# A hybrid decoder layer on one core: VectorE's order fixed by hand between the output projection and the FFN's block sums

## Chip, cores, metric

The kernel runs on one core of one Trainium2 chip. The metric is the device time of one execution in microseconds (us). Engines are named as in the profile: PE is TensorE (matmuls), PEld its weight loads, DVE is VectorE, ACT is ScalarE, POOL is GpSimd, SP is SyncE, whose only work here is to start DMAs. ACTq and SPq are the DMAs that those engines start.

## The reference

One layer of a decoder over 1024 prompt tokens and 8 x 4 sample tokens. Cut to what matters here:

```python
h = rmsnorm(x, g_pre); p = h @ w_in              # all mixers' columns in one projection
# ya: gated short conv, yb: windowed attention, yc: chunked spatial gate
merged = g[:, :, 0] * (ya @ w_ba) + g[:, :, 1] * (yb @ w_bb) + g[:, :, 2] * (yc @ w_bc)
x = x + rmsnorm(merged @ w_o, g_post)            # output projection, second norm, residual
up = rmsnorm(x, g_pre_f) @ w_up                  # FFN
upc, ffn_new = causal_dwconv(up, ffn_prev, conv_f_w, conv_f_b)
fa, fb = jnp.split(upc, 2, axis=-1)
x = x + rmsnorm((jax.nn.silu(fa) * fb) @ w_down, g_post_f)
```

`rmsnorm(x, g)` is `x * rsqrt(mean(x*x) + 1e-6) * g`. The model width is 1024, the FFN's inner width 2816, all in float32.

## The kernel before

Features lie on the 128 partitions, tokens along the free dimension: 1056 tokens (1024 + 32), cut into three chunks `c` of 352. `M8` holds eight feature tiles of 1056 tokens in float32. Every product is made of three matmuls of rounded values: each operand is split into a high part (a rounded copy, made by ACT) and a low part (the rest, a subtraction on DVE); `H` holds the 8 high and 8 low tiles of the activations. Weights come in blocks of 4 tiles (128 x 512): SP loads a block into a `raw` buffer (three of these), ACT copies it, DVE subtracts. Up-projection weights of the first FFN columns go into slots of `Y`, which hold output-projection weights until PE is through with these.

The place in question is the passage from the output projection to the FFN:

- For each chunk, the output projection makes eight tiles `n`, 24 matmuls each. `evac_o` lets ACT move a tile out of PSUM (scaled by `g_post`) and square it; DVE adds up the squares.
- `chain(c, ...)` is then the whole norm, residual and second norm of chunk `c`. It is a generator that is advanced by one step after every 12 matmuls of the following work. Its parts: `rstd_of` adds squares over partitions with small matmuls against `ones` (tile `aux`); `factor_of` scales the sums on DVE and raises them to -1/2 on POOL (tile `rs`, 88x4); `spread` sends these back over the partitions by four transposes on PE, and ACT copies the result (`rs`, later `R`). Then, for pairs of tiles n = 0, 2, 4, 6: DVE multiplies `M` by `rs`, DVE adds the residual `xr` (loaded from `in_x`), ACT squares, DVE adds the squares to `acc2`, and the sum goes to DRAM (`x2d`). A second `rstd_of` reads `acc2`; after its `spread` DVE scales by `g_pre_f` and `R`, ACT copies to `H`, DVE subtracts.
- Chunk 0's chain runs beside chunk 1's output projection, chunk 1's beside chunk 2's. Chunk 2's runs beside the first FFN products (`up_unit` for j = 0 and 1), with tiles cut out of the `cz` buffers in place of its own, and with two residual buffers. Chunk 1 of the FFN products follows chunk 0, then chunk 2.
- `combos(X, p)` makes the block sums for the Strassen products of the later FFN columns (sums of quarters of `M`, four high and four low parts in `Y`), for two halves p of the tokens. `act_pair(j)` is the convolution, the SiLU and the product of FFN column pair j. Weights of the Strassen columns are loaded into `M` when the block sums are through with it.

PE's order is the order in which the program is written. The order of the other engines, and of the DMAs on each queue, is chosen by a scheduler from its own estimate of the times; each engine then runs its row strictly in that order, and a row's wait holds everything behind it.

## Time and profile before

| | us |
|---|---|
| runs (three) | 1490.8, 1488.62, 1488.98 |
| median | 1488.98 |
| profiled execution | 1487.42 |
| its span in the profile | 1485.6 |

The span runs from the first to the last instruction; 1.8 us of the profiled execution lie around it. "PE aux L100" is the group of small matmuls of `rstd_of`, "PE aux L306" the transposes of `spread`. A timeline row reads: start, duration of the group, engine, line, operation, out<-in, shape, count, and in brackets the idle time of the engine before it and what ended it. A row of the view by stretches gives the stretch, its length, busy time and instruction count of PE, PEld, DVE, ACT and POOL, then the granted clock of PE (1.00 is full speed), the busy share of the DMA engines and GB/s.

### The profile page before, as it was taken

The numbers are of one execution on the slowest core, as the hardware profiler recorded it, in microseconds if no ns is written. First come the engines' busy times: TensorE is split into PE (matmuls) and PEld (weight loads), VectorE is DVE, ScalarE is ACT, GpSimd is POOL, SyncE is SP. The second block draws the span as 40 slices with busy tenths as digits, with TensorE's granted clock in tenths as the row PEclk, the third lists the DMA queues.
The fourth block names the chain that finished last, engine by engine and source line by source line (L and its number), as shares of the span: only waits on it lengthen the run. The fifth ranks groups of instructions, "written<-read, shape, count | busy, mean of one in ns | idle before, by whom it ended". The sixth has DMA issues, their size and how long they took to land.

```text
span 1485.6 us, 25718 instructions
## 1 busy us (share of the span) xinstructions
PE 1434.6 (97%) x10163; PEld 1424.2 (96%) x10163; DVE 900.3 (61%) x1603; ACT 658.0 (44%) x1338; POOL 251.2 (17%) x319
## 2 busy tenths in 40 slices
PE   4899999999999999999889999999999999999997
PEld 3899999999999999999889999999999999999997
DVE  6844445325777546755678677777777783453546
ACT  5444444445766322243436454555454574121333
POOL 2100000012455215410013022122122210000000
PEclk9999999999999999999999999999999999999998
DMA  6222333211001236642340122221222174231215
GB/s 231 77 91 96 102 108 109 91 55 36 30 30 36 59 119 181 188 141 79 122 138 38 57 81 80 87 80 66 79 80 80 54 261 148 73 109 43 86 39 151
DMA packets 77833, 141.40 MB, mean 95 GB/s; under 512 B 8256, under 2 KB 34816, under 8 KB 77696
## 3 DMA queue, kind: packets, MB, share of 16 engines
q1 hardware_dynamic: 66192, 112.94, 24.0%
q10 hardware_dynamic: 11520, 26.82, 4.7%
q8 instruction: 80, 1.31, 0.4%
q14 instruction: 41, 0.34, 0.1%
HBM read 105.58 MB, written 35.16 MB: 95 GB/s over the span
## 4 chain that ended last, share of the span: by engine, by line
PE 90%; DVE 3%; ACT 2%; issue 2%; POOL 1%; DMA 1%; SPq 0%; POOLq 0%; DVEq 0%; ACTq 0%
PE mm L100 54%; PE wb L100 20%; PE aux L100 13%; POOL rs L301 1%; DVE M L94 1%; PE sp L100 1%; ACT M L686 1%; DMA M<-in_x 1%; PE aux L699 1%; DVE M L680 0%; DMA raw<-in_wu 0%; DVE Y L97 0%; PE aux L306 0%; DVE H L97 0%; DVE acc L94 0%
## 5 line engine op out<-in xcount | busy, mean ns | idle before, releaser
L100 PE MATMUL mm<-Y,wh 128*128 128x264 f32 (+1 forms) x1824 | 364.2, 295 | 0.0
L100 PE MATMUL mm<-H,wh 128*128 128x352 f32 (+1 forms) x1568 | 354.5, 313 | 1.5 <-DVE Y L97 0.9
L100 PEld LDWEIGHTS mm<-Y,wh 128*128 128x128 f32 x1824 | 292.3, 189 | 0.0
L100 PE MATMUL mm<-Y,wl 128*128 128x264 f32 (+1 forms) x912 | 268.7, 295 | 0.0
L100 PEld LDWEIGHTS mm<-H,wh 128*128 128x128 f32 x1568 | 261.6, 188 | 2.5 <-PE aux L100 1.1
L100 PE MATMUL mm<-H,wl 128*128 128x352 f32 (+1 forms) x784 | 243.5, 311 | 0.0
L100 PEld LDWEIGHTS mm<-Y,wl 128*128 128x128 f32 x912 | 171.2, 188 | 0.0
L91 ACT ACTIVATE wh<-M 128x512 fp32r<-128x512 f32 x126 | 79.6, 632 | 155.0 <-PE aux L100 67.4
L100 PE MATMUL wb<-H,wh 128*128 128x264 f32 (+1 forms) x720 | 147.6, 298 | 0.0
L100 PEld LDWEIGHTS mm<-H,wl 128*128 128x128 f32 x784 | 147.2, 188 | 0.0
L91 ACT ACTIVATE wh<-raw 128x512 fp32r<-128x512 f32 (+1 forms) x98 | 58.2, 594 | 169.3 <-PE mm L100 109.6
L1035 DVE SCALAR_TENSOR_TENSOR cz<-U,cst,cz 128x1072 f32<-128x1072 f32 x88 | 113.9, 1329 | 13.4 <-ACT cz L1033 13.3
L100 PEld LDWEIGHTS wb<-H,wh 128*128 128x128 f32 x720 | 116.3, 188 | 0.0
L100 PE MATMUL mm<-H,Y 128*128 128x352 f32 x624 | 109.4, 335 | 2.6 <-DVE H L97 2.6
L97 DVE TENSOR_TENSOR wl<-M,wh 128x512 fp32r<-128x512 f32 x126 | 86.4, 686 | 39.0 <-ACT wh L91 39.0
L100 PEld LDWEIGHTS mm<-H,Y 128*128 128x128 f32 x624 | 105.4, 196 | 3.0 <-DVE H L97 3.0
L100 PE MATMUL wb<-H,wl 128*128 128x264 f32 (+1 forms) x360 | 107.2, 298 | 0.0
L97 DVE TENSOR_TENSOR wl<-xraw,wh 128x512 fp32r<-128x512 f32 x70 | 48.5, 692 | 90.0 <-ACT wh L91 89.5
L301 POOL TENSOR_TENSOR rs<-rs,nhalf 88x4 f32<-88x4 f32 (+2 forms) x12 | 24.7, 2055 | 395.7 <-DVE rs L300 395.7
L94 DVE TENSOR_TENSOR M<-M 128x512 f32<-128x512 f32 (+1 forms) x88 | 69.5, 790 | 26.7 <-DMA M<-in_wu 25.9
L94 DVE TENSOR_TENSOR M<-mm,M 128x352 f32<-128x352 f32 (+3 forms) x79 | 39.5, 505 | 76.0 <-PE mm L100 76.0
L97 DVE TENSOR_TENSOR wl<-raw,wh 128x512 fp32r<-128x512 f32 (+1 forms) x72 | 52.7, 733 | 52.3 <-ACT wh L91 52.3
(219 smaller groups left out, 2636.2 us busy)
## 6 DMA issues: line engine op xcount, KB each, us to landing
M<-in_wu SPq DMA_DIRECT2D x72, 256.0 KB, 2.6
sig<-sigd SPq DMA_DIRECT2D x72, 176.0 KB, 2.9
y2d<-cz ACTq DMA_DIRECT2D x22, 528.0 KB, 2.8
sigd<-M ACTq DMA_DIRECT2D x40, 264.0 KB, 3.3
xraw<-in_win SPq DMA_DIRECT2D x40, 256.0 KB, 2.7
raw<-in_wd SPq DMA_DIRECT2D x40, 256.0 KB, 2.7
raw<-in_win SPq DMA_DIRECT2D x39, 256.0 KB, 2.6
Y<-y2d SPq DMA_DIRECT2D x14, 528.0 KB, 6.6
```

Source lines behind the costliest of these rows:

```text
L91: act.activation(out, in_, AF.Copy)
L94: return eng.tensor_tensor(out, a, b, op=op)
L97: eng.tensor_tensor(out, a, b, op=ALU.subtract)
L100: pe.matmul(out, lhsT, rhs, start=start, stop=stop, skip_group_check=more)
L301: pool.tensor_tensor(v, v, nhalf[:bs, :nb], op=ALU.pow)
L686: act.activation(s[:, h, :], s[:, h, :], AF.Exp, bias=ng[:, h : h + 1], scale=SCALE, accum_out=l[:, h : h + 1])
L699: pe.transpose(pt[:, h * P : (h + 1) * P], s[:, h, kb * P : (kb + 1) * P], ident)
L1035: dve.scalar_tensor_tensor(z, u[:, s : s + CONV], cwf[:, f, s : s + 1], z, ALU.mult, ALU.add)
```

## The change

From the output projection until the second half of the block sums, DVE's instructions stand in the order in which the program is written, as PE's do already. With that, the written order is altered in a few places: `combos` becomes a generator in four pieces, of which the first half's two pieces fill the places behind the two `rstd_of` of chunk 2, and the rest comes after that chain; `act_pair(1)` comes after the second half. Behind each power on POOL a DVE copy (`ru`) is made, and the transposes read the copy. The residual of chunks 0 and 1 is loaded into four buffers ahead of the chunk's products; in chunk 2 the later two residual loads, and all the stores to `x2d`, go out on ACT's queue. Squares are made per tile (352) and not per pair (704), and the buffers `sq` and `sq2` go from two to one.

```diff
@@ combos
             tt(b11, b12, b11, ALU.subtract)
             tt(b12, b22, b12, ALU.subtract)
+            yield
             tt(b22, b22, b11, ALU.subtract)
             part(1, b22)
+            yield
             part(0, b11)
             part(2, b12)
+            yield
             tt(b21, b21, b22, ALU.subtract)
             part(3, b21)
@@ factor_of
             pool.tensor_tensor(v, v, nhalf[:bs, :nb], op=ALU.pow)
+            if hold[0]:
+                u = fixed.tile([P, 4], F32, name="ru", bufs=2)[:bs, :nb]
+                dve.tensor_copy(u, v)
+                v = u
@@ evac_o
-                    sq = pc.tile([P, CW], F32, name="sq", bufs=2)
+                    sq = pc.tile([P, CW], F32, name="sq", bufs=1)
...
-                        sums[c] = pc.tile([P, 2, CW], F32, name="sq2", bufs=2)
+                        sums[c] = pc.tile([P, 2, CW], F32, name="sq2", bufs=1)
@@ chain
-            load_xr(0)
-            load_xr(2)
+            queue = nc.sync if c < 2 else nc.scalar
             yield
             spread = rstd_of(acc, rs)
+            next(fill, None)
...
-                tt(m, m, xr[n // 2 % 2], ALU.add)
-                load_xr(n + 4)
-                if n == 0:
-                    act.activation(acc2, m, AF.Square)
-                elif type(sq) is list:
+                tt(m, m, xr[n // 2], ALU.add)
+                queue.dma_start(x2d[:, n : n + 2, cc(c)], m)
+                if c == 2 and n < 4:
+                    load_xr(c, n + 4, xr[n // 2], queue)
+                for q in range(2):
+                    if n == 0:
+                        act.activation(acc2[:, q, :], m[:, q, :], AF.Square)
+                    else:
+                        act.activation(sq[q], m[:, q, :], AF.Square)
+                if n:
                     for q in range(2):
-                        act.activation(sq[q], m[:, q, :], AF.Square)
                         tt(acc2[:, q, :], acc2[:, q, :], sq[q], ALU.add)
-                else:
-                    act.activation(sq, m, AF.Square)
-                    tt(acc2, acc2, sq, ALU.add)
-                nc.sync.dma_start(x2d[:, n : n + 2, cc(c)], m)
...
             spread = rstd_of([acc2[:, 0, :], acc2[:, 1, :]], R[:, cc(c)])
+            next(fill, None)
...
         steps = []
+        order = ExitStack()
+        order.enter_context(tc.manual_schedule(engines={mybir.EngineType.DVE}))
+        hold[0] = True
         for c in CHUNKS:
+            if c < 2:
+                xr = [pc.tile([P, 2, CW], F32, name="xr", bufs=4) for _ in range(4)]
+                for n in range(0, 8, 2):
+                    load_xr(c, n, xr[n // 2])
...
-                    if c == 2:
+                    if c == 2 and j == 0:
                         act_pair(j)
-            combos(M8, 1)
+            drain(combos(M8, 1))
+            act_pair(1)
+            order.close()
+            hold[0] = False
```

Scaling and splitting for `H` is also written one pair ahead (`scale(n + 2)` before the subtraction of pair n).

What the engines' rows become is shown at three places. First, DVE in chunk 1's chain. Before (`Y<-raw,Y` is the subtraction of a weight block, `R<-R,sq` a sum of chunk 2's squares, `acc` here the second sum of squares):

```order
L94 TENSOR_TENSOR M<-M,rs 128x2x352 x4
L97 TENSOR_TENSOR Y<-raw,Y 128x512
L94 TENSOR_TENSOR M<-M,xr 128x2x352 x2
L97 TENSOR_TENSOR Y<-raw,Y 128x512
L94 TENSOR_TENSOR R<-R,sq 128x352
L97 TENSOR_TENSOR Y<-raw,Y 128x512
L94 TENSOR_TENSOR acc_7577<-acc_7577,sq_7578 128x704
L94 TENSOR_TENSOR M<-M,xr 128x2x352
```

The same place after the change:

```order
L94 TENSOR_TENSOR M<-M,rs 128x2x352
L94 TENSOR_TENSOR M<-M,xr 128x2x352
L97 TENSOR_TENSOR Y<-raw,Y 128x512 x2
L94 TENSOR_TENSOR M<-M,rs 128x2x352
L94 TENSOR_TENSOR M<-M,xr 128x2x352
L94 TENSOR_TENSOR acc_7599<-acc_7599,sq_7597 128x352 x2
L94 TENSOR_TENSOR R<-R,sq 128x352
L94 TENSOR_TENSOR M<-M,rs 128x2x352
L94 TENSOR_TENSOR M<-M,xr 128x2x352
L94 TENSOR_TENSOR acc_7599<-acc_7599,sq_7597 128x352 x2
L97 TENSOR_TENSOR Y<-raw,Y 128x512 x2
```

Each pair is finished before the next begins, and the first two weight subtractions, which stood ahead of the chain, stand behind its first pair.

Second, ACT at the end of that chain, after the change (`sq_7597<-M` are the squares of pairs n = 4 and n = 6, `M<-mm` and `sq<-mm` chunk 2's tiles):

```order
L941 ACTIVATE sq_7597<-M 128x352 x2
L898 ACTIVATE M<-mm,cst 128x352
L91 ACTIVATE Y<-raw 128x512
L941 ACTIVATE sq_7597<-M 128x352 x2
L91 ACTIVATE wh<-raw 128x512
```

A weight block's copy stands ahead of the last pair's squares. Third, DVE in chunk 2's chain; before (`M<-M 128x4x264` and `Y<-M,Y` belong to the block sums, `M<-M 128x512` to later weights):

```order
L97 TENSOR_TENSOR Y<-M,Y 128x1056
L94 TENSOR_TENSOR M<-M 128x4x264
L97 TENSOR_TENSOR Y<-M,Y 128x1056
L94 TENSOR_TENSOR M<-M,cz 128x2x352 x4
L97 TENSOR_TENSOR Y<-M,Y 128x1056
L94 TENSOR_TENSOR M<-M,cz 128x2x352 x2
L94 TENSOR_TENSOR M<-M 128x512
L94 TENSOR_TENSOR cz<-cz 128x352
```

and after:

```order
L310 TENSOR_SCALAR rs<-aux 88x4
L314 COPY ru<-rs 88x4
L94 TENSOR_TENSOR M<-M 128x4x264 x2
L94 TENSOR_TENSOR M<-M,cz 128x2x352 x4
L94 TENSOR_TENSOR cz<-cz 128x352 x2
L94 TENSOR_TENSOR M<-M,cz 128x2x352 x2
L94 TENSOR_TENSOR cz<-cz 128x352 x2
L97 TENSOR_TENSOR wl<-raw,wh 128x512
L94 TENSOR_TENSOR M<-M,cz 128x2x352 x2
L94 TENSOR_TENSOR cz<-cz 128x352 x2
```

Only two block sums stand ahead of the chain, and its four rows `M<-M,cz ... x4` are now multiply, add, multiply, add, where they were four multiplications.

## The prediction

> **What bounds the kernel now.** I read the page first, then who waited for whom on PE between 690 and 800 us, then PE's timeline there with the granted clock, and last the rows of DVE, ACT and the DMAs ahead of each wait.

> ```profile
> PE 1434.6 (97%) x10163; PEld 1424.2 (96%) x10163; DVE 900.3 (61%) x1603; ACT 658.0 (44%) x1338; POOL 251.2 (17%) x319
> ```

> PE is the bound. The change gives PE the same row of instructions as before, so it can only move PE's waits, and the clock behind them. In the stretch it touches these are:

> ```profile
> PE aux L100 <- DVE acc L94: 4.6, 2, 3.9
> PE aux L100 <- issue: 3.8, 1, 3.8
> PE aux L100 <- DVE R L94: 0.2, 1, 0.2
> ```

> That is 8.55 us, all in front of the matmuls against `ones`. In PE's timeline:

> ```profile
> 693.45 1.41 PE L100 MATMUL aux<-ones,acc 128*88 128x1 f32 x16 [0.66 <-DVE acc L94]
> ...
> 709.25 4.12 PE L100 MATMUL wb<-H,Y 128*128 128x352 f32 x24
> ...
> 725.22 2.10 PE L100 MATMUL wb<-H,Y 128*128 128x352 f32 x12
> 731.22 2.48 PE L100 MATMUL aux<-ones,acc 128*88 128x1 f32 x16 [3.90 <-DVE acc L94]
> 733.56 6.13 PE L100 MATMUL wb<-H,Y 128*128 128x352 f32 x24
> ...
> 762.67 5.99 PE L100 MATMUL mm<-H,Y 128*128 128x352 f32 x36
> 772.41 2.60 PE L100 MATMUL aux<-ones,cz 128*88 128x1 f32 x16 [3.75 <-issue]
> 774.88 5.97 PE L100 MATMUL mm<-H,Y 128*128 128x352 f32 x24
> ```

> The waits of 0.66, 3.90 and 3.75 us belong to the second sums of chunks 0, 1 and 2. The reader is to see also what follows the long ones: the 16 small matmuls take 2.48 and 2.60 us where 1.41 do behind the short wait, the 24 matmuls behind them 6.13 and 5.97 us where 4.12 do. The clock says why:

> ```profile
> 734.00:736.00 2.00, 2.00 (x8) 2.00 (x8) 0.00 (x0) 0.00 (x0) 0.97 (x1) 0.50 0.07 25
> ...
> 776.00:778.00 2.00, 2.00 (x9) 2.00 (x8) 0.00 (x0) 0.00 (x0) 0.37 (x1) 0.50 0.00 0
> ```

> In these stretches, behind both long waits, PE ran at 0.50 (the third last column); behind the wait of 0.66 us the 16 small matmuls took 1.41. So each long wait cost its length and a slow stretch: 1.07 + 2.01 = 3.08 us for chunk 1, 1.19 + 1.85 = 3.04 for chunk 2. All that can be won here is 8.55 + 6.12 = 14.7 us; PE has no other wait in this passage.

> **Chunk 0's chain.** Its last sum was 0.66 us late. With the pairs finished one by one and all residuals loaded ahead, the last pair's sum follows the last square with nothing queued between; I count the wait as gone: 0.66 us won (between 0 and 0.66).

> **Chunk 1's chain.** The rows that set its pace:

> ```profile
> 715.15 3.29 DVE L94 TENSOR_TENSOR M<-M,rs 128x704 f32<-128x704 f32 x4
> 718.36 0.69 DVE L97 TENSOR_TENSOR Y<-raw,Y 128x512 fp32r<-128x512 f32 x1
> 718.96 1.69 DVE L94 TENSOR_TENSOR M<-M,xr 128x704 f32<-128x704 f32 x2
> ...
> 724.87 0.89 DVE L94 TENSOR_TENSOR M<-M,xr 128x704 f32<-128x704 f32 x1 [1.77 <-DMA xr<-in_x]
> 763.91 0.87 ACT L926 ACTIVATE cz<-M 128x352 f32<-128x352 f32 x2
> 768.95 0.96 DVE L94 TENSOR_TENSOR cz<-cz 128x352 f32<-128x352 f32 x2 [0.62 <-ACT cz L926]
> 722.32 0.63 ACT L91 ACTIVATE Y<-raw 128x512 fp32r<-128x512 f32 x1
> raw<-in_wu SPq DMA_DIRECT2D x9, 256.0 KB, 3.6
> DMA to landing us min/median/max: 2.4/3.6/6.4
> ```

> Before, the chain lost 1.77 us to a residual that landed late; the four buffers take that away. But the new order puts waits in its place. A multiplication or addition of a pair takes 0.82 us (3.29 / 4), so 1.64 a pair; a weight subtraction 0.60 (718.36 to 718.96); a residual sum of chunk 2 0.44; and from a finished addition to finished squares and their sums it is half of the 0.87, the 0.96 and the hand-overs, 1.5 us. In the row before, DVE filled these 1.5 us with the next pair. Now it stands still in them, three times. And two more things queue up. The first weight subtractions stood ahead of the chain, in DVE's idle time, and now stand behind the first pair; the buffer that they free is the one into which SP loads weight block 5, whose copy ACT makes ahead of the squares of pair 2. In the same way the copy of block 7 stands ahead of the squares of pair 6, and its load waits for a subtraction that follows the sums of pair 4.

> With loads of 2.4 us (the shortest) the times are: start 715.2, as before; pair 0 ends 716.8; two weight subtractions, 718.0, the first of them at 717.5 frees the buffer; block 5 lands 719.9, is copied by 720.5; squares and sums of pair 2 by 722.0; sum of chunk 2, 722.4; pair 4, 724.0; its sums 725.5; weight subtraction 726.1, block 7 lands 728.5, copied 729.1; pair 6 was added by 728.4, so its squares start at 729.1 and the sums end at 730.6. With the median of 3.6 us for both loads it is 1.2 us more at each, 733.1. PE is free at 727.3 (725.22 + 2.10), so it waits 3.3 to 5.8 us; I take the middle, 4.6, against 3.90 before: 0.7 lost. That is long enough for the clock to fall as it did before, so nothing is won behind it.

> **The first sum of chunk 2** (0.24 us, the row of 0.2 above) waited for DVE's last sum of squares, behind block sums. These are now behind it: 0.2 won.

> **Chunk 2's chain.**

> ```profile
> 754.56 0.47 PE L306 MATMUL aux<-ident,rs 88*128 88x88 f32 x4
> 755.11 0.46 ACT L91 ACTIVATE cz<-aux 128x352 f32<-128x352 f32 x1
> 756.89 3.29 DVE L94 TENSOR_TENSOR M<-M,cz 128x704 f32<-128x704 f32 x4
> 760.10 1.24 DVE L97 TENSOR_TENSOR Y<-M,Y 128x1056 fp32r<-128x1056 f32 x1
> 761.27 1.68 DVE L94 TENSOR_TENSOR M<-M,cz 128x704 f32<-128x704 f32 x2
> 749.86 0.36 ACTq L973 DMA_DIRECT2D sff<-in_sff  x1
> cz<-in_x SPq DMA_DIRECT2D x4, 352.0 KB, 5.0
> ```

> Before, `rs` was there at 755.57, the first multiplication began at 756.89, and the first additions, which free the residual buffers, at 761.27, behind four multiplications and a block sum; the loads behind them then took 5.0 us, in the company of the weight loads. Now pair 0 is multiplied and added by 755.6 + 1.64 = 757.2. Stores and residual loads cost ACT an issue each, 0.36 us by the one ACT issue shown: load 4 leaves by 758.0 and, even at 5.0 us, is there at 763.0. Pair 2 is added by 758.9, but ACT has two issues and pair 0's squares (0.72 + 0.87) first, to 758.8, then its own two issues: squares start at 759.7, sums end at 761.2. Pair 4: added by 763.8 (load 763.0, addition 0.82); one store, squares, sums: 0.36 + 1.5, 765.7. A weight subtraction, pair 6, a store, squares and sums: 0.6 + 1.64 + 0.36 + 1.5, so 769.8. PE is free at 768.7 (762.67 + 5.99): a wait of about 1.2 us where 3.75 stood, between 0 (the load in less than 5.0 us, which the weight loads no longer crowd since the block sums that free their room come later) and 2.9 (ACT's copies of block sums and evacuations each in front). That is 2.55 won, and at 1.2 us the clock stays up, as it did after 0.66: 3.04 more.

> **The rest**, at nothing, with its cover. The copies behind the powers: 24 matmuls lie between the small matmuls and the transposes, 4.12 us by the row of 709.25, and

> ```profile
> 775.37 1.00 POOL L301 TENSOR_TENSOR rs<-rs,nhalf 88x4 f32<-88x4 f32 x1 [17.54 <-DVE rs L300]
> ```

> the power takes 1.00 of them, so a copy of some tenths is in time; DVE, which stands for that 1.00 in front of the copy, has only what the sums above contain behind it. The block sums moved behind chunk 2's chain: four rows of 1.24 for the first half and eight for the second, 15 us, and two convolution pairs. behind the second transposes of chunk 2 PE still has 12 + 24 matmuls of chunk 1, 96 of chunk 2 and 144 of FFN column 2 before the first Strassen product needs them, 276 at 4.12 per 24, some 45 us, and DVE is busy 61% of its time; without that cover each us late would be one on PE.

> **The sum:** 0.66 - 0.7 + 0.2 + 2.55 + 3.04 = 5.75 us. Against the profiled execution, 1487.42, this is 1481.7. The median of the runs is 1.56 us above that execution, so against the median 1488.98 it is 1483.2. What a measurement can tell from no change here is 0.2%, 3.0 us.

> **Rivals.**

> The clock. Each of two waits above 3.7 us brought it down, none below 0.7 did; the rows show nothing between. If chunk 1's wait comes out near 3.3 us and the clock holds, 3.08 more is won: 1480.1. For it speaks the shortest load, against it that both waits near that length did fall. [...]

> The wait moves, and nothing is won. Chunk 1 at its far end, 5.8 us, chunk 2 at 2.9 with the 16 small matmuls behind it slow enough that the clock falls again: 5.8 + 3.08 + 2.9 + 3.04 = 14.8, just what is lost now, 1489.0; with only the clock of chunk 2 falling, 1486.2. For it speaks that ACT now has evacuations, copies, issues and squares of chunk 2 in one row.

> Slower: the weights of chunk 0's output projection.

> ```profile
> 641.96 0.80 SPq L906 DMA_DIRECT2D xr<-in_x  x2
> 650.82 11.84 PE L100 MATMUL mm<-H,Y 128*128 128x352 f32 x72
> 652.68 0.63 ACT L91 ACTIVATE Y<-raw 128x512 fp32r<-128x512 f32 x1 [0.37 <-DMA raw<-in_wo]
> ```

> Tile 3's matmuls end at 654.75 (a third of 11.84 after 650.82) and tile 5's begin at 658.7. The sum of tiles 2 and 3 (an addition of 704, 0.89 as in the row of 724.87) now stands in front of the weight subtractions for tile 5, and needs tile 3's square, about 1.0 after its end (two ACT rows of about half a us, as 0.46 above): 655.8 + 0.9 + 0.69 = 657.4, a margin of 1.3 us; for tile 7 it is the same again. Ahead of all this SP starts four residual loads, not two, 704 KB more in front of the weights. The margin is gone once ACT's copies, which stand ahead of tile 3's evacuation and wait for loads, are 1.3 us late. Late by 5 us, it would be 3.7 us at tile 5, with a slow clock of 3.1 behind, and some 2 at tile 7: 8.8 lost, 1483.2 + 8.8 = 1492. It decides from 5.75 us on. Against it speaks that the copies wait 0.37 us only for a load at 652.68.

> **Chances.** The forecast, chunk 2's wait mostly gone and chunk 1's kept: 0.52, by its own bounds (3.3 to 5.8, 0 to 2.9) 1480.7 to 1486. The clock holds at chunk 1: 0.16, near 1480. The wait moves: 0.21, 1486 to 1489. Slower: 0.11. Left out on both sides is a fifth at most with 1478.5 to 1489.5. Faster by over 0.2% (below 1486.0) are the first two and a quarter of the third: 0.73. Within 0.2%: the rest of the third and a little of the last: 0.17. Slower: 0.10.

> **What would show it.** After the change the second sum of chunk 0 should have no wait; that of chunk 1 a wait of 3.3 to 5.8 us behind DVE's `acc`, a clock of 0.50 after it, and ACT's last squares there directly behind a `Y<-raw` copy that waits for `raw<-in_wu`; that of chunk 2 a wait under 3 us with the clock at 1.00 behind it. PE should have no wait for `H`, `Y` or `wl` from 640 to 830 us. The prediction is wrong if chunk 1's wait is under 2.5 us (the weight loads then don't hold the squares), if chunk 2's stays above 3, or if a new wait stands in the output projection of chunk 0 or at the first Strassen product.

## The result and the profile after

Beside the first runs of the changed kernel the kernel before took 1488.8 us (median of 4 runs) and the changed kernel 1479.8 (4 runs, 1479.45 to 1479.92), a ratio of 0.9942 with a 95% interval of 0.9927 to 0.9957. In a second lot, timed beside the experiments, it took 1482.09 us (6 runs, 1479.99 to 1484.15) against 1488.79: 0.9955, 0.9941 to 0.9969. So it is 6.7 to 9.0 us faster, where 5.75 were forecast. What was expected of the second lot, ahead of it: a median of 1480 to 1483 with a spread of several us if the 1479.8 us were in part luck of those four runs, all runs within 1 us of 1479.8 if not. The first came out. The profiled execution took 1479.45 us with a span of 1477.7; that of before had 1487.42.

TensorE's row on the page after, and who waited for whom on PE from 640 to 830 us (total, times, longest):

```profile
PE 1430.0 (97%) x10163; PEld 1419.4 (96%) x10163; DVE 903.0 (61%) x1615; ACT 659.0 (45%) x1347; POOL 248.4 (17%) x319
```

```profile
PE aux L100 <- DVE acc L94: 4.9, 2, 4.7
PE aux L100 <- issue: 0.6, 1, 0.6
```

PE's timeline, at the places that the prediction showed of before:

```profile
673.27 0.71 PE L100 MATMUL aux<-ones,acc 128*88 128x1 f32 x8
...
691.72 1.51 PE L100 MATMUL aux<-ones,acc 128*88 128x1 f32 x16
...
707.41 0.76 PE L100 MATMUL aux<-ones,acc 128*88 128x1 f32 x8 [0.24 <-DVE acc L94]
...
730.75 2.56 PE L100 MATMUL aux<-ones,acc 128*88 128x1 f32 x16 [4.68 <-DVE acc L94]
733.17 5.93 PE L100 MATMUL wb<-H,Y 128*128 128x352 f32 x24
...
748.94 0.71 PE L100 MATMUL aux<-ones,R 128*88 128x1 f32 x8
...
761.55 5.98 PE L100 MATMUL mm<-H,Y 128*128 128x352 f32 x36
768.18 1.64 PE L100 MATMUL aux<-ones,cz 128*88 128x1 f32 x16 [0.64 <-issue]
769.68 4.13 PE L100 MATMUL mm<-H,Y 128*128 128x352 f32 x24
```

The second sum of chunk 0 has lost its wait of 0.66 us. Chunk 1's wait has grown from 3.90 to 4.68, with slow matmuls behind it as before (2.56 and 5.93 us). Chunk 2's has shrunk from 3.75 to 0.64, and the 24 matmuls behind it take 4.13 us where they took 5.97: the clock stayed up. The wait of 0.24 us at the first sum of chunk 2 is gone, and one of the same length stands at the first sum of chunk 1. In the clock's view (PEclk is the third last column) the slow stretch behind chunk 1 is still there and the one behind chunk 2 is not:

```profile
734.00:736.00 2.00, 2.00 (x9) 0.50 0.49 164
...
776.00:778.00 2.00, 2.00 (x14) 1.00 0.00 0
```

Chunk 1's chain ahead of the long wait, first on ACT's timeline, then on DVE's:

```profile
729.03 0.63 ACT L91 ACTIVATE Y<-raw 128x512 fp32r<-128x512 f32 x1 [3.50 <-DMA raw<-in_wu]
729.57 0.87 ACT L941 ACTIVATE sq<-M 128x352 f32<-128x352 f32 x2
```

```profile
730.08 0.96 DVE L94 TENSOR_TENSOR acc<-acc,sq 128x352 f32<-128x352 f32 x2 [1.45 <-ACT sq L941]
```

The last squares stand directly behind a weight copy that waited 3.50 us for its load, the sums follow, and PE's small matmuls begin right behind these.

### The profile page after: what moved, and what is told of

Read it like the earlier page. It is cut to its first block, busy times and chain, and to the rows that moved or that the text cites. A ratio compares the mean times of both kernels' runs of the same rounds, so it can differ in the third digit from the quotient of the medians.

```text
span 1477.7 us, 25715 instructions
## 1 busy us (share of the span) xinstructions
PE 1430.0 (97%) x10163; PEld 1419.4 (96%) x10163; DVE 903.0 (61%) x1615; ACT 659.0 (45%) x1347; POOL 248.4 (17%) x319
## 4 chain that ended last, share of the span: by engine, by line
PE 90%; DVE 4%; ACT 2%; issue 2%; POOL 1%; DMA 1%; ACTq 0%; SPq 0%; POOLq 0%; DVEq 0%
PE mm L100 54%; PE wb L100 20%; PE aux L100 13%; DVE M L94 1%; POOL rs L311 1%; PE sp L100 1%; ACT M L700 1%; PE aux L713 1%; DMA M<-in_x 1%; DVE M L694 0%; DMA raw<-in_wu 0%; DVE acc L94 0%; DVE Y L97 0%; ACT Y L91 0%; PE aux L320 0%
## 5 line engine op out<-in xcount | busy, mean ns | idle before, releaser
L100 PE MATMUL mm<-Y,wh 128*128 128x264 f32 (+1 forms) x1824 | 363.8, 295 | 0.0
L100 PE MATMUL mm<-H,wh 128*128 128x352 f32 (+1 forms) x1568 | 354.3, 313 | 1.5 <-DVE Y L97 0.9
L100 PEld LDWEIGHTS mm<-Y,wh 128*128 128x128 f32 x1824 | 292.6, 188 | 0.0
L100 PE MATMUL mm<-Y,wl 128*128 128x264 f32 (+1 forms) x912 | 269.4, 295 | 0.0
L100 PEld LDWEIGHTS mm<-H,wh 128*128 128x128 f32 x1568 | 261.6, 188 | 2.5 <-PE aux L100 1.1
L100 PE MATMUL mm<-H,wl 128*128 128x352 f32 (+1 forms) x784 | 243.7, 311 | 0.0
L100 PEld LDWEIGHTS mm<-Y,wl 128*128 128x128 f32 x912 | 171.8, 188 | 0.0
L100 PE MATMUL wb<-H,wh 128*128 128x264 f32 (+1 forms) x720 | 147.7, 298 | 0.0
L91 ACT ACTIVATE wh<-M 128x512 fp32r<-128x512 f32 x126 | 79.5, 631 | 152.8 <-PE aux L100 65.9
L100 PEld LDWEIGHTS mm<-H,wl 128*128 128x128 f32 x784 | 147.3, 188 | 0.0
L91 ACT ACTIVATE wh<-raw 128x512 fp32r<-128x512 f32 (+1 forms) x98 | 58.3, 594 | 169.2 <-PE mm L100 110.6
L100 PEld LDWEIGHTS wb<-H,wh 128*128 128x128 f32 x720 | 116.4, 188 | 0.0
L100 PE MATMUL mm<-H,Y 128*128 128x352 f32 x624 | 107.2, 331 | 2.6 <-DVE H L97 2.6
L100 PE MATMUL wb<-H,wl 128*128 128x264 f32 (+1 forms) x360 | 107.3, 298 | 0.0
L97 DVE TENSOR_TENSOR wl<-M,wh 128x512 fp32r<-128x512 f32 x126 | 86.5, 686 | 32.8 <-ACT wh L91 32.8
L100 PEld LDWEIGHTS mm<-H,Y 128*128 128x128 f32 x624 | 103.1, 192 | 3.0 <-DVE H L97 3.0
L97 DVE TENSOR_TENSOR wl<-xraw,wh 128x512 fp32r<-128x512 f32 x70 | 48.5, 693 | 90.3 <-ACT wh L91 89.8
L94 DVE TENSOR_TENSOR M<-mm,M 128x352 f32<-128x352 f32 (+3 forms) x79 | 39.5, 506 | 76.2 <-PE mm L100 76.2
L94 DVE TENSOR_TENSOR M<-M 128x512 f32<-128x512 f32 (+1 forms) x88 | 69.5, 790 | 27.1 <-DMA M<-in_wu 26.3
L97 DVE TENSOR_TENSOR wl<-raw,wh 128x512 fp32r<-128x512 f32 (+1 forms) x72 | 53.0, 737 | 51.7 <-ACT wh L91 51.7
## 6 DMA issues: line engine op xcount, KB each, us to landing
M<-in_wu SPq DMA_DIRECT2D x72, 256.0 KB, 2.6
xraw<-in_win SPq DMA_DIRECT2D x40, 256.0 KB, 2.7
raw<-in_wd SPq DMA_DIRECT2D x40, 256.0 KB, 2.6
raw<-in_win SPq DMA_DIRECT2D x39, 256.0 KB, 2.6
```

What stands on the lines that cost most here:

```text
L91: act.activation(out, in_, AF.Copy)
L94: return eng.tensor_tensor(out, a, b, op=op)
L97: eng.tensor_tensor(out, a, b, op=ALU.subtract)
L100: pe.matmul(out, lhsT, rhs, start=start, stop=stop, skip_group_check=more)
```

## The experiments

The runs share one table. "Stretch" is the time from the start of chunk 0's first sum to that of the kernel's last sum of squares on PE: 674.12 to 1474.32 before, 673.27 to 1466.74 after. It leaves out what happens ahead of it, and with that the output projection of chunk 0, where weights can come late (see the rivals below). A lot is one chip: versions 1 to 4 ran on one, the second lot with 5, 6 and 8 on another, 4 again with 7 and 9 on a third, 10 on a fourth. Each ratio is to the kernel before in the same lot.

```
version                        median us  ratio to before (95%)   stretch  wait chunk 1  waits chunk 2
before                         1488.5 to 1489.1                   800.20   3.90          0.24, 3.75
changed, second lot            1482.09    0.9955 (0.9941-0.9969)  793.36   4.37          0, 0.63
1 no order                     1485.03    0.9971 (0.9957-0.9985)  798.57   2.08 + 1.26   2.63, 2.68, 1.70
2 order for chunk 1 only       1488.34    0.9996 (0.9986-1.0007)  798.48   4.53          2.63, 2.68, 0.23
3 order for chunk 2 only       1477.39    0.9920 (0.9904-0.9936)  790.67   1.80 + 0.39   0, 0.63
4 no copies                    1484.47    0.9975 (0.9964-0.9987)  795.18   4.79          0, 0.58
4 no copies, again             1484.54    0.9970 (0.9955-0.9985)  794.16   4.34          0, 0.58
5 weights first                1480.31    0.9944 (0.9932-0.9956)  793.15   4.01          0, 0.63
6 weights late                 1483.11    0.9962 (0.9950-0.9974)  795.80   2.05          2.90, 0.64
7 SyncE's queue for chunk 2    1481.29    0.9952 (0.9934-0.9969)  792.57   4.80          0, 0
8 loads only                   1487.12    0.9992 (0.9976-1.0008)  799.82   2.11 + 1.26   2.58, 2.18
9 weights first, pipelined     1472.79    0.9898 (0.9875-0.9921)  786.02   0             0, 0.63
10 pipelined                   1475.48    0.9911 (0.9892-0.9931)  788.15   0.74          0, 0.64
```

The waits are those of PE at the second sum of chunk 1; and at the first sum, the transposes (where they waited) and the second sum of chunk 2.

**1. Without VectorE's order.**

```diff
-        order.enter_context(tc.manual_schedule(engines={mybir.EngineType.DVE}))
```

> The changed kernel without VectorE's emission order; the copies behind the powers, the four residual buffers and the ScalarE queue of chunk 2 stay. Theory A (the gain comes from VectorE's order in chunk 2's chain, pairs finished one by one): the wait in front of the second sum of chunk 2 is back at about 3.7 us with the clock at 0.50 behind it, chunk 1's wait stays near 4, and the time is 1486 to 1489. Rival B (the gain comes from where the residuals are loaded and on whose queue): chunk 2's wait stays under 1.5 us, the clock stays up there, and the time is 1479 to 1481.

1485.03 us: against the second lot, 3 us of the changed kernel's gain in time and 5.2 of the 6.8 in the stretch are gone. That is 1 us below the least of theory A. Chunk 2's loss did not come back as one wait at the second sum but as three:

```profile
PE aux L100 <- DVE acc L94: 3.3, 2, 2.1
PE aux L320 <- DVE ru L314: 2.7, 1, 2.7
PE aux L100 <- DVE R L94: 2.6, 1, 2.6
PE aux L100 <- issue: 1.7, 1, 1.7
```

The second row is new. VectorE's rows there show what the copy behind a power costs without the order:

```profile
754.59 0.15 DVE L310 TENSOR_SCALAR rs<-aux 88x4 f32<-88x4 f32 x1
754.66 2.42 DVE L97 TENSOR_TENSOR Y<-M,Y 128x1056 fp32r<-128x1056 f32 x2
758.42 0.17 DVE L314 COPY ru<-rs 88x4 f32<-88x4 f32 x1 [1.34 <-POOL rs L311]
...
760.55 4.89 DVE L94 TENSOR_TENSOR M<-M,cz 128x704 f32<-128x704 f32 x6
```

The scheduler put block sums ahead of the statistics and again between the statistics and the copy, and took all four multiplications ahead of the third addition. Two of the three waits, 2.63 and 2.68 us, stand behind block sums, and only the last, 1.70, behind the pairs. Theory A named the right place and a wrong form. Rival B is out.

**2 and 3. The order for one chain alone.** In 2 the order ends behind the output projection, in 3 it begins there.

```diff
         pcs.close()
+        order.close()
```

```diff
-        order.enter_context(tc.manual_schedule(engines={mybir.EngineType.DVE}))
         ...
         pcs.close()
+        order.enter_context(tc.manual_schedule(engines={mybir.EngineType.DVE}))
```

> The emission order holds for the output projection and chunk 1's chain alone and ends before chunk 2's. Theory A: chunk 1's wait is that of the changed kernel (4.7 us), chunk 2's is back at 3 to 4 us with the slow clock of 3 us behind it: 6 us slower than the changed kernel, about 1486. Rival B: no difference from the changed kernel, 1480.

> The emission order begins only behind chunk 1's chain and holds for chunk 2's alone. Theory A: chunk 2's wait is under 1 us as in the changed kernel; in chunk 1 the scheduler puts the weight subtractions ahead of and between the pairs, so the loads that ScalarE's copies wait for start earlier, but the pairs' additions come after all multiplications: a wait of 2.5 to 4.5 us. Time 1477 (if the clock holds there) to 1481. Rival C (what is won in chunk 2 depends on chunk 1's chain being in order too, since the two share ScalarE): chunk 2's wait is over 2 us and the time is over 1484.

With the order for chunk 1 alone nothing is left of the gain (0.9996; 1488.34 us is 2 us above theory A, and chunk 2's loss has the form of version 1, not that of one wait). With the order for chunk 2 alone the gain is larger than the whole change's: 1477.39 us, with all six runs (1471.94 to 1478.53) below all ten of the changed kernel, and the stretch 2.7 us shorter than in the changed kernel's second profile. PE's waits of version 3:

```profile
PE aux L100 <- DVE acc L94: 2.2, 2, 1.8
PE aux L100 <- issue: 0.6, 1, 0.6
```

Chunk 2's wait is the changed kernel's, chunk 1's is 2.2 us, a little below the 2.5 to 4.5 that were expected, where the order makes 4.4 to 4.7. So the order wins in chunk 2 and loses in chunk 1. With the rest of the change kept, it loses 2.2 to 2.5 us of wait there; the 0.5 to 0.8 us by which the changed kernel stands behind the kernel before are what the rest of the change left of it. Rival C is out. What the order does in chunk 2 is two things, the pairs one by one and the block sums moved behind them, and no run has one without the other.

**4. Without the copies behind the powers**, run twice.

```diff
-        hold[0] = True
```

> The changed kernel without the copy behind each power. By the prediction each copy (0.17 us on VectorE, behind a power of about 1 us) lies beside matmuls and costs nothing: within 0.5 us of the changed kernel. Rival D: the copies do work for the chain, since they make VectorE stand still for the power where it would otherwise go on; without them some sums of squares shift, and chunk 1's or chunk 2's wait changes by 0.5 to 1.5 us.

> The version without the copies once more. Its PE waits were those of the changed kernel within 0.1 us and its median was 2.4 to 4.7 us above; the profiled run had two or three slow windows of the clock more. Theory: the copies cost and win nothing, and which of the short waits meet the end of a clock window changes from run to run; the median here is 1480 to 1484 and the spread reaches below 1482. Rival D: the copies are worth 2 to 4 us; the median is again 1484 or more, and none of the runs is below 1482.

As the prediction had it, PE's waits in the changed stretch are the changed kernel's: none is more than 0.5 us from those of its two profiles, which differ by 0.3 us themselves. The medians are not: 1484.47 and 1484.54, 2.4 to 4.7 us above the changed kernel, and 3.3 above version 7, which has the copies and was timed beside the second of them. The second time single runs reach down to 1478.88, which rival D excludes; the median is what rival D says. Much of what the profiles show of the difference lies ahead of the changed stretch: the first sum of chunk 0 starts at 678.03 and 678.15 here, at 673.27 and 675.96 in the changed kernel's profiles. Such a late start needs no missing copies: version 7, which has them, starts it at 678.08.

One part does go with the copies. From the last transposes of chunk 2 to the kernel's last sum of squares, where the clock stays up in all of these profiles, PE takes 693.64 us in every profile without copies (before, 780.68 to 1474.32; both of version 4; version 8) and 693.09 to 693.20 in all ten with them (changed kernel, 773.64 to 1466.74). These 0.54 us can come from the copies or from the small buffers `ru` that they bring along; no run tells which, or why. That the copies also shift some slow stretch of the clock (below) is possible and wasn't shown. What they are worth beyond the 0.54 us stays open.

**5 and 6. The weight blocks of chunk 2's output projection**, made ahead of the pair that they followed (5), or two blocks ahead of chunk 1's chain and four behind it (6).

```diff
-                for _ in products(8, Hhi, Hlo, evac_o(n, acc), (c,), pieces=wow + 2 * n):
+                for q, _ in enumerate(products(...)):
+                    if c == 2 and n < 4 and q == 1:
+                        limit[0] = upw + 2 * n + 2 if n < 3 else 1 << 30
+                        make(min(limit[0], upw + 8))
```

```diff
+                    if c == 2 and n == 1 and q == 1:
+                        limit[0] = upw + 4
+                        make(limit[0])
         ...
+                if c == 2 and n == 5:
+                    limit[0] = 1 << 30
+                    make(upw + 8)
```

> The changed kernel, with each pair of weight blocks of chunk 2's output projection made ahead of the pair of chunk 1's chain that it now follows. Theory A (chunk 1's wait is the chain addition, weight subtraction, load of the next weight block, ScalarE's copy, squares): the subtractions free the buffers one pair (1.6 to 3 us) earlier, and chunk 1's wait falls from 4.7 to between 1.5 and 3 us; the time is 1 to 6 us below the changed kernel's, by whether the clock still falls. Rival B (the wait is VectorE's own work, three pairs finished one by one): the wait stays at 4.5 or grows by 0.6 to 1.2, since more stands ahead of the pairs.

> The changed kernel, with weight blocks 2 and 3 of chunk 2's output projection ahead of chunk 1's first pair, and blocks 4 to 7 only behind its last sums, so that one ScalarE copy at most stands ahead of the squares. Theory A: the last sums end at about 725.5, before PE is free at 726, and chunk 1's wait falls from 4.7 us to under 0.5 with the clock at 1.00 behind it: 4.7 + 1.1 + 1.8 = 7.6 us below the changed kernel, if the late weights don't keep PE waiting (the next products that need them start at about 733). Rival B (VectorE's own work makes the wait): it stays above 3 us. Rival C: the wait moves to the late weights, 1 to 4 us in front of a matmul on Y between 733 and 750.

Version 5's wait of 4.01 lies between the two expectations: earlier subtractions alone give some 0.5 us. ScalarE's waits for the loads ahead of the squares of chunk 1's chain fall from 2.49 and 3.50 us to 0.74 and 0.32, but VectorE still stands still for squares three times (1.77, 1.34 and 0.62 us; 2.32, 0.62 and 1.45 in the changed kernel), and the same four subtractions still stand ahead of its last sums. Its 1480.31 us can't be told from the 1482.09 of the changed kernel beside it (intervals 0.9932 to 0.9956 and 0.9941 to 0.9969). Version 6 halves the wait to 2.05 us, neither theory A's 0.5 nor rival B's 3, so of the 4.4 to 4.7 us about half was the weight blocks: ScalarE's copies with their loads and VectorE's subtractions together. But version 6 is not faster, 1483.11: the wait moved, as rival C says in kind, to another place. PE's rows:

```profile
728.74 1.60 PE L100 MATMUL aux<-ones,acc 128*88 128x1 f32 x16 [2.05 <-DVE acc L94]
730.20 5.66 PE L100 MATMUL wb<-H,Y 128*128 128x352 f32 x24
...
748.80 0.76 PE L100 MATMUL aux<-ones,R 128*88 128x1 f32 x8 [2.90 <-DVE R L94]
749.42 5.67 PE L100 MATMUL mm<-H,Y 128*128 128x352 f32 x24
...
769.62 1.65 PE L100 MATMUL aux<-ones,cz 128*88 128x1 f32 x16 [0.64 <-issue]
771.12 5.65 PE L100 MATMUL mm<-H,Y 128*128 128x352 f32 x24
```

PE didn't wait for the late weights, but for the first sum of chunk 2, whose squares' sums now stand on VectorE behind the late subtractions. And the clock fell three times, behind 2.05, 2.90 and even 0.64 us.

**7. SyncE's queue for chunk 2's stores and residuals.**

```diff
-            queue = nc.sync if c < 2 else nc.scalar
+            queue = nc.sync
```

> The changed kernel with chunk 2's stores and later residual loads issued by SyncE, not ScalarE. Theory: ScalarE saves two to eight issues of 0.4 to 0.5 us ahead of the squares, SyncE issues them behind nothing else that is late; chunk 2's wait stays between 0 and 1 us, and the time is within 2 us of the changed kernel's 1480 to 1482. Rival B (ScalarE's queue is what wins in chunk 2): the residuals of pairs 4 and 6 land 2 us or more later, the wait is back above 2 us, and the time is 1484 or more.

1481.29 us, in the bounds of theory. Chunk 2's second sum has no wait at all here, so ScalarE's queue wins nothing; its issues cost the 0.63 us of wait that are left there.

**8. The loads alone**: neither the order nor the copies.

```diff
-        order.enter_context(tc.manual_schedule(engines={mybir.EngineType.DVE}))
-        hold[0] = True
```

> The changed kernel without the emission order and without the copies behind the powers: what is left of the change is where the residuals are loaded, ScalarE's queue for chunk 2, and the squares in single steps. Theory A: the wait of 2.7 us for the copied power that the version without the order shows is gone, chunk 1's wait is 2 to 3.5 us, chunk 2's 1.5 to 4 us; the time is 1482 to 1486. Rival: the order gives nothing and the loads all of it, 1479 to 1481.

1487.12 us, 0.9992: no difference from before that could be told. The wait for the copied power is gone, as expected; chunk 2 waits 2.58 + 2.18 us. Residual buffers, queue and single squares give nothing that shows without the order; the time is above theory A's 1486. Against version 1, taking the copies away removed the wait of 2.68 us and won no time: the second sum of chunk 2 waits 0.5 us longer (2.18 for 1.70), the clock also falls behind the wait of 2.58 us, for 6.8 us (752.9 to 759.75), and the stretch is 1.3 us longer (799.82 for 798.57).

**9 and 10. The sums behind the next pair.** In chunks 0 and 1 a pair's squares go into its residual buffer, and their sums follow the next pair's addition; 9 has the weights of version 5 too, 10 those of the changed kernel.

```diff
+                s = sq if c == 2 else [xr[n // 2][:, 0, :], xr[n // 2][:, 1, :]]
...
-                if n:
+                late.append((n, s))
+                while late and (c == 2 or n == 6 or late[0][0] < n):
+                    k, s = late.pop(0)
+                    if k:
                     for q in range(2):
-                        tt(acc2[:, q, :], acc2[:, q, :], sq[q], ALU.add)
+                        tt(acc2[:, q, :], acc2[:, q, :], s[q], ALU.add)
```

> The version with the weight blocks first, and in chunks 0 and 1 the additions of a pair's squares now follow the next pair's multiplication and addition (the squares are kept in the pair's residual buffer). Theory A (of the 4.7 us of chunk 1's wait some 2.3 are ScalarE's weight copies and some 2.0 VectorE standing still for squares between pairs, as the version with the late weights has it): both are covered now, the last sums end at about 727.8 us where PE is free at 726.7, a wait of about 1.1 us, 3 us less than with the weights first alone; time 1474 to 1479, by whether the clock falls behind it. Rival B (VectorE's sheer work sets it): the wait stays at 3 to 4 us and the time at 1480.

> The changed kernel with the sums of squares put behind the next pair in chunks 0 and 1, and the weight blocks where the changed kernel has them. Theory A1 (VectorE standing still between pairs is the larger part, and the weight copies then lie beside its work): chunk 1's wait is 0 to 1.5 us and the time 1472 to 1478. Theory A2 (the weight copies hold the squares by themselves, and only both steps together take the wait away): the wait is 2 to 3.5 us, the clock falls behind it, and the time is 1478 to 1481.

Version 9 takes 1472.79 us, faster than both kernels: its slowest run, 1476.17, is below the fastest of either. Its wait is not 1.1 us but none, and the clock stays up at both places:

```profile
725.43 1.60 PE L100 MATMUL aux<-ones,acc 128*88 128x1 f32 x16
726.89 4.12 PE L100 MATMUL wb<-H,Y 128*128 128x352 f32 x24
```

VectorE has no gap left between the pairs; its rows run on, the multiplication, the addition, the sums of the pair before:

```profile
719.44 0.88 DVE L94 TENSOR_TENSOR M<-M,rs 128x704 f32<-128x704 f32 x1
720.36 0.89 DVE L94 TENSOR_TENSOR M<-M,xr 128x704 f32<-128x704 f32 x1
721.17 0.95 DVE L94 TENSOR_TENSOR acc<-acc,xr 128x352 f32<-128x352 f32 x2
722.04 0.88 DVE L94 TENSOR_TENSOR M<-M,rs 128x704 f32<-128x704 f32 x1
722.96 0.89 DVE L94 TENSOR_TENSOR M<-M,xr 128x704 f32<-128x704 f32 x1
723.76 1.95 DVE L94 TENSOR_TENSOR acc<-acc,xr 128x352 f32<-128x352 f32 x4
```

Version 10 has 0.74 us of wait left and 1475.48 us: theory A1. With the sums one pair later the weight copies lie beside VectorE's work; without that, the two ways of moving the weights that were tried (5 and 6) took half of the wait at most.

## Why the prediction was right, and where its sizes were off

Its mechanisms held but for one, the reason why the clock stays up behind chunk 2. Its sum of 5.75 us stands against 5.9 between the two profiles, in part because its errors cancel (0.56 us too little for chunk 2's wait, 0.24 too much for the clock behind it and 0.2 too much for its first sum); by its own terms:

- Chunk 0: 0.66 us, measured 0.66.
- Chunk 1: -0.7, measured -0.78, and -0.47 in the second profile. The forecast 4.6 us stands against 4.68 and 4.37, behind ACT's copy, with the slow clock behind it (0.12 us less of it). Both ends of this wait came more than 1 us earlier than forecast: PE was free at 726.07 (730.75 - 4.68) and not at 727.3, and started again at 730.75, where the middle of the forecast was 731.9. The forecast kept the places of before, but the whole passage had moved up (the chain's first multiplication began at 713.92 for 715.2), so the difference was right. Versions 5, 6, 9 and 10 show both of its parts to be real: VectorE's standing still between pairs and the weight blocks.
- The first sum of chunk 2: 0.2 won, but the same 0.24 came up at chunk 1's first sum, which the prediction did not look at. Net nothing.
- Chunk 2's wait: 2.55, measured 3.11. The term was mis-sized, most of all by the residual loads. The prediction took 5.0 us as before; with no weight load issued between 749.2 and 764.9 us they took

```profile
cz<-in_x ACTq DMA_DIRECT2D x2, 352.0 KB, 3.7
```

  and pair 4's addition didn't wait for them. That takes 1.0 us off the forecast chain. As an estimate from VectorE's rows, its other steps took some 0.8 us more than their terms (4.28 us from the end of pair 4's sums to that of pair 6's, 764.23 to 768.51, where 4.1 were forecast), and PE started at 768.18, behind the first of the last two sums, where the prediction let it wait for both. Versions 2 and 3 show that this gain is the order's, versions 7 and 8 that it isn't the queue's or the loads'.
- The clock behind chunk 2: 3.04, measured 2.80 (8.57 us for the 16 and 24 matmuls before, 5.77 after). The size is right for this execution, but the step's reason failed. It said that the clock stays up because a wait of 1.2 us is near 0.66. In versions 6 and 10 it fell behind the same wait of 0.64 us (5.65 us for the 24 matmuls); and "nothing between" 0.7 and 3.7 us held for the rows shown only, since before has a wait of 1.90 us near 448 us (last section) behind which the clock stayed up. PE's rows of version 10, to be read beside the 768.18 and 769.68 of the changed kernel:

```profile
764.19 1.65 PE L100 MATMUL aux<-ones,cz 128*88 128x1 f32 x16 [0.64 <-issue]
765.69 5.65 PE L100 MATMUL mm<-H,Y 128*128 128x352 f32 x24
```

  Between the changed kernel's execution and version 6's, with the same wait and the same small matmuls, the place of these on the grid of the clock's changes differed (last section); version 10's grid is not shown. So the term is 2.80 us in this execution and 1.3 by the rows of versions 6 and 10 (8.57 less 1.65 + 5.65), and that it came out at nearly its full size here was luck.

The rest of the distance to 9.0 us is not in these terms. The profiled executions differ by 7.97 us: 0.85 ahead of chunk 0's first sum (0.46 of it the wait for the first loads, 14.96 against 14.50 us), 6.73 in the stretch, of which 5.9 are named above and 0.54 lie behind chunk 2's last transposes and go with the copies (version 4) while 0.3 stay unnamed, and 0.39 behind the last sum. The second lot's 6.7 us, with 6.84 in the stretch, say that the first four runs of the changed kernel fell well: in ten runs it spread from 1479.45 to 1484.15. The first median, 1479.8, is even outside the forecast's own 1480.7 to 1486 and where the rival with the held clock stood, near 1480; it is the traces, not the times, that decide between the two.

The rivals. The clock held at chunk 1 in neither profile of the changed kernel, nor in any other behind a wait of 3.9 us or more. That the wait moves and nothing is won didn't happen in the changed kernel; version 6 shows that it was near. The weights of chunk 0's output projection came in time in both profiles of the changed kernel, to within 0.3 us (the 48 matmuls at this place took 8.00 and 8.20 us; 7.94 before). Versions 2, 4, 6 and 10, written alike there, show PE waiting for them in some executions, for 0.22 to 0.72 us; this is version 10:

```profile
668.59 3.83 PE L100 MATMUL wb<-H,Y 128*128 128x352 f32 x22 [0.70 <-DVE Y L97]
```

So that margin was as thin as the 1.3 us of the prediction said, and far from the 5.75 us that would have decided.

## What to carry to other kernels

An order written by hand should leave work between an operation and the result of another engine that it needs: the written order won 3 us of wait where the scheduler had filled VectorE with work that nobody needed yet, and lost 2.2 to 2.5 where it had filled it with the next pair; with the sums one pair later the second wait went too. How much of the 3 us is the pairs and how much the block sums is an estimate only: before, the first multiplication began 1.3 us after `rs` was there (756.89 for 755.57), behind a block sum, and after, at once. A hand-over through a copy cost no wait here in the fixed order, and one of 2.68 us where the scheduler was free to queue other work ahead of the copy. And a short wait can cost more than its length: behind the same 0.64 us the clock stayed up in the changed kernel's execution and fell in those of versions 6 and 10, where the 24 matmuls took 5.65 us for 4.13. So compare versions by waits and a stretch of the trace as well as by medians.

## What the runs showed of the hardware

```profile
51.90:52.00 0.10, 0.10 (x2) 0.82 0.00 0
...
731.10:731.20 0.10, 0.00 (x0) 0.94 0.73 274
```

In the same way the falls of version 6 at 730.30 and 771.26 us are 40.96 us or 12 steps apart. The grid's place differed between executions: the falls at chunk 1 in the changed kernel's two profiles, at 730.36 and 733.23 us, are 2.87 us apart, no whole number of steps. Version 6, the granted clock on both sides of each change:

```profile
730.10:730.30 0.20, 0.20 (x4) 1.00 0.00 0
730.40:730.60 0.20, 0.20 (x2) 0.50 0.00 0
733.40:733.60 0.20, 0.20 (x2) 0.50 0.00 0
733.80:734.00 0.20, 0.20 (x3) 1.00 0.00 0
750.50:750.70 0.20, 0.20 (x3) 1.00 0.86 211
750.90:751.10 0.20, 0.20 (x2) 0.50 0.94 366
...
771.00:771.20 0.20, 0.20 (x5) 1.00 0.00 0
771.40:771.60 0.20, 0.20 (x2) 0.50 0.33 72
```

The changes at about 733.7, 750.8 and 771.3 us are 1, 6 and 12 steps of 3.41 behind the first, at 730.3. In the step that ended with the fall at 771.3 PE waited 0.64 us, ran the 16 one-column matmuls for 1.50, and full ones for the rest. In the first profile of the changed kernel, where the clock stayed up behind the same wait, 11 steps from its fall at 730.4 us put the edge of a step, as an estimate from that grid, at 767.9, in the middle of the wait, so that no step held more than 1.8 us of the 2.1 us of waiting and small matmuls. The slow step in version 6 cost about 1.5 us (5.65 against 4.13). The same wait of 1.90 us near 450 us, in a part that no version touches, left the clock up in the kernel before (the first two fences, PE's timeline and the clock's view behind it) and in version 1 the clock fell behind it (the other two):

```profile
448.01 0.63 PE L699 MATMUL aux<-ident,M 128*128 128x128 f32 x4 [1.90 <-DVE M L94]
```

```profile
450.00:452.00 2.00, 2.00 (x18) 1.00 0.00 0
```

```profile
449.32 0.71 PE L713 MATMUL aux<-ident,M 128*128 128x128 f32 x4 [1.90 <-DVE M L94]
```

```profile
450.00:452.00 2.00, 2.00 (x9) 0.50 0.00 0
```

That falls like these, in one execution and not in another, make part of the spread of the kernel before, 1482.17 to 1492.75 us over all lots, is the author's estimate. The clock fell behind waits of 0.64, 1.90 and 2.05 us, all shorter than a step of 3.41 us, so PE ran matmuls in part of the step ahead of each of these falls. Behind waits of over 3.7 us in the changed passage it stayed up in no profile; there were eight at chunk 1 alone, of 3.90 to 4.80 us.
